# Four leading units instead of three in the gate/up stage of a two-layer trunk, with their first weights fetched and rounded inside the projection ahead

## The chip, the cores and the metric

The kernel runs on one NeuronCore of a Trainium2 chip. The time is device time of one execution in microseconds, the median of several. The engines are named as in the profile: PE (TensorE, matmuls), PEld (its weight loads), DVE (VectorE), ACT (ScalarE), POOL (GpSimd), SP (SyncE, which issues nearly all loads from HBM).

## The reference, cut to what matters

```
D_MODEL, SEQ, DEPTH, D_FF = 1024, 512, 2, 2816          # float32 throughout
def swiglu(x, w_gate, w_up, w_down):
    h = silu(x @ w_gate) * (x @ w_up)
    return h @ w_down
def reference(x, ...):
    h = x
    for i in range(DEPTH):
        m = diff_attention(h, ...) if i % 2 == 0 else short_gated_conv(h, ...)
        h = layer_norm(ALPHA * h + m, ln1_g[i], ln1_b[i])
        h = layer_norm(ALPHA * h + swiglu(h, w_gate[i], w_up[i], w_down[i]), ln2_g[i], ln2_b[i])
    return h
```

Each mixer ends in a projection of 1024 x 1024 (`wo` in layer 0, `wco` in layer 1), a residual and a layer norm. What follows it, gate and up of the SwiGLU, is what the change touches, in both layers.

## The kernel before, in words

Every matmul is done as three: an operand is split into a rounded part `hi` and the remainder `lo`, and hi·hi, hi·lo and lo·hi are added up in PSUM. So every weight tile is loaded raw and then made into a pair `whi`, `wlo`.

Gate and up run in 11 units (`UNITS`). A unit is one block of the Strassen-Winograd scheme: 7 products, 24 matmuls each (`product`, L580-L589), into three PSUM banks. Bank x takes x11·w11 and then x12·w21. Bank y takes s2·t2, s3·t3 and x22·t4. Bank z takes s1·t1 and s4·w22. The left factors (x11, x12, s1 to s4, x22) are made once in a layer from the normalized rows; w11, w12, w21, w22 are the four blocks of the unit's weights, and t1 to t4 are sums of them.

Two ways lead to a pair. A plain block (11, 21, 22) is loaded; ACT copies it to `whi` (L564) and its negative to `wlo` (L565), and POOL issues a DMA that adds the raw block to `wlo` (L566, called the accumulate below), after which `wlo` holds the remainder with its sign turned. A combined block (t1 to t4) is a sum on DVE (L576); ACT rounds it (L57), and DVE takes the remainder (L58).

The buffers are rings. Raw blocks 11 and 22 have three places (`raw`), 12 and 21 have two (`raw2`), `whi` and `wlo` have six each. The next load into a place waits until whatever read the old content is done; for a plain block that is the landing of its accumulate. SP issues loads strictly in its order, so a load that waits for its place holds those behind it.

The projection (`project_norm`, L203) works on four row tiles of 128 (tt = 0 to 3). The last four weight groups of its second half run tile by tile (L252), so that a tile's residual, norm and transposes can start while the next tile is multiplied. A `turn` (L168 to L198) transposes one row tile on PE (L175) and makes its part of the left factors on ACT and DVE: tiles 0 and 1 give x11 and x12, tiles 2 and 3 all the others, which need both halves. The turns of tiles 2 and 3 are left over to the next stage.

That stage (`swiglu`, L539) has `LEAD` = 3 leading units: for u = 0, 1, 2 the load of w11, the product x11·w11 and the copy `e` of bank x (`start`, L600, L608), with the turns of tiles 2 and 3 behind u = 0 and u = 1; then for the three units x12·w21 and a silu (`second`, L611); then the other five products of each (`rest`, L615). Units 3 to 10 do all seven products in one go. What stands after the leads is set by the order in which the kernel's text issues it and by a scheduler that orders each engine's list; the lists quoted below are what came out.

Of the kernel before, what the change touches and what calls it, by code (L numbers as in the profile page):

```python
# [35 lines left out]
LEAD = 3  # L36
# [3 lines left out]
def trunk(ctx: ExitStack, tc: tile.TileContext, t: dict):  # L40
# [113 lines left out]


# [12 lines left out]
    def turn_forms(tt, r, x, name):  # L168
# [20 lines left out]
        nc.scalar.copy(c, tps[0])  # L189
        nc.vector.tensor_tensor(d, a, tps[0], op=ALU.subtract)  # L190
        nc.vector.tensor_tensor(c, c, tps[1], op=ALU.add)
        form("s1", c)
        form("x22", tps[1])
        nc.vector.tensor_tensor(a, c, a, op=ALU.subtract)
        form("s2", a)
        form("s3", d)
        nc.vector.tensor_tensor(b, b, a, op=ALU.subtract)
        form("s4", b)  # L198
# [4 lines left out]
    def project_norm(lhs, w, kt, gb, xT, out, name, early=None):  # L203
# [335 lines left out]
    def swiglu(i, x, turns, open_next, out):  # L539
# [3 lines left out]
        with ExitStack() as fctx:  # L543
            wk = fctx.enter_context(tc.tile_pool(name=f"gu{i}", bufs=1, reuse_waits="tile"))

            def blocks(u, keys):
                out = {}
                for key in keys:
                    a, b = int(key[0]) - 1, int(key[1]) - 1
                    tag, pool, n = ("raw", wpool, 3) if a == b else ("raw2", wk, 2)  # L550
                    raw = pool.tile([P, 4, 256], F32, tag=tag, name=f"raw_gu{i}_{u}_{key}", bufs=n)
                    nc.sync.dma_start(raw, t["wgu"][i, u, a, b])
                    out[key] = raw
                return out

            def pair(name):
                hi = wpool.tile([P, 4, 256], F32R, tag="whi", name=f"whi_{name}")
                lo = wpool.tile([P, 4, 256], F32R, tag="wlo", name=f"wlo_{name}")
                return hi, lo


            def plain(raw, name):
                hi, lo = pair(name)
                nc.scalar.copy(hi, raw)  # L564
                nc.scalar.activation(lo, raw, AF.Copy, scale=-1.0)  # L565
                nc.gpsimd.dma_start(lo, raw, accum_op=ALU.add)  # L566
                return hi, lo
# [28 lines left out]
            def hidden(u):  # L596
                pool = slots["x"] if u >= UNITS - 4 else slots["xa"]
# [2 lines left out]
            def start(u, raw):  # L600
# [1 line left out]
                product(s["x"], plain(raw["11"], f"gu{i}_{u}_11"), "x11", True)
                if u < LEAD:
# [192 lines left out]
```

## Time and profile before

| | |
|---|---|
| median of 3 runs | 1150.58 us (1150.36 to 1151.18) |
| the profiled execution | 1150.07 us, span in the trace 1148.3 us |
| PE busy | 1119.0 us, 97% of the span |
| PEld / DVE / ACT / POOL busy | 999.1 / 737.4 / 520.8 / 119.6 us |
| PE clock granted, mean | 0.99 |
| accumulates `wlo_gu<-raw_gu` | 66, 512 KB each, median 5.8 us from issue to landing |
| loads `raw_gu<-in_wgu` | 100, 512 KB each, median 4.6 us |

Times in the rows are microseconds from the start of the span. A timeline row begins with start and duration; the bracket at its end, where there is one, holds how long the engine had stood idle before it and what ended that. In the rows of windows PEclk is the granted clock of TensorE (1.00 is 2.4 GHz, 0.50 is 1.2 GHz).

### The profile page before, as it was taken

How to read it: one execution, taken by the hardware profiler on the slowest of the kernel's cores; microseconds unless marked ns; L12 is line 12 of the kernel's file. 1: busy time of each engine (PE TensorE's matmuls, PEld its weight loads, DVE VectorE, ACT ScalarE, POOL GpSimd, SP SyncE). 2: the span in 40 equal slices, each digit the busy share in tenths (PEclk: the TensorE clock that was granted, in tenths of full speed). 3: DMA queues.
4: the chain of work that ended last, by engine and by line, in shares of the span. 5: the costliest groups of instructions: out<-in, count | busy, mean ns of one | idle time of the engine just before them, and what ended most of it. 6: DMA issues, size and time to landing. Idle time of an engine off the chain costs nothing.

```text
span 1148.3 us, 17876 instructions
## 1 busy us (share of the span) xinstructions
PE 1119.0 (97%) x7242; PEld 999.1 (87%) x7242; DVE 737.4 (64%) x1065; ACT 520.8 (45%) x790; POOL 119.6 (10%) x149
## 2 busy tenths in 40 slices
PE   9999999996999999999999999999899999999997
PEld 7877787786999999988889888889799999988886
DVE  7787877576986776832355544447897767682416
ACT  5554646536565655721212333225655565651210
POOL 1111112120011111000010000012001111100002
PEclk9999999998999999999999999999899999999998
DMA  8521222247788777533313423355778787743302
GB/s 290 178 74 37 74 60 89 76 111 199 189 204 194 173 201 176 150 96 106 111 56 111 146 92 92 94 155 120 216 196 193 177 191 186 164 137 101 106 24 74
DMA packets 44739, 155.58 MB, mean 135 GB/s; under 512 B 5200, under 2 KB 6096, under 8 KB 44656
## 3 DMA queue, kind: packets, MB, share of 16 engines
q1 hardware_dynamic: 35152, 119.83, 33.8%
q0 software_dynamic: 9504, 34.61, 16.5%
q8 instruction: 57, 0.93, 0.3%
q14 instruction: 26, 0.21, 0.1%
HBM read 117.72 MB, written 2.10 MB: 104 GB/s over the span
## 4 chain that ended last, share of the span: by engine, by line
PE 81%; DVE 6%; issue 4%; ACT 3%; DMA 3%; POOL 1%; SPq 0%; POOLq 0%; DVEq 0%; ACTq 0%
PE y L588 15%; PE z L588 10%; PE x L588 9%; PE o_dn L77 7%; PE o_dn L76 7%; PE o_dn L75 7%; PE in L75 4%; PE in L77 4%; PE in L76 4%; DMA wlo_gu<-raw_gu 2%; ACT p L426 1%; PE o_wco L75 1%; PE o_wco L77 1%; PE o_wco L76 1%; DVE nm L423 1%
## 5 line engine op out<-in xcount | busy, mean ns | idle before, releaser
L58 DVE TENSOR_TENSOR wlo_gu_t<-gu_t,whi_gu_t 128x1024 fp32r<-128x1024 f32 x88 | 106.9, 1221 | 30.4 <-ACT whi_gu_t L57 30.2
L58 DVE TENSOR_TENSOR wlo_dn<-raw_dn,whi_dn 128x1024 fp32r<-128x1024 f32 x44 | 53.6, 1222 | 112.6 <-ACT whi_dn L57 112.4
L57 ACT CAST whi_gu_t<-gu_t 128x1024 fp32r<-128x1024 f32 x88 | 90.9, 1047 | 75.3 <-DVE gu_t L576 29.6
L75 PE MATMUL o_dn<-whi_dn,hid 128*128 128x512 f32 (+1 forms) x320 | 123.8, 387 | 0.0
L77 PE MATMUL o_dn<-whi_dn,hid 128*128 128x512 f32 (+1 forms) x320 | 123.8, 387 | 0.0
L76 PE MATMUL o_dn<-wlo_dn,hid 128*128 128x512 f32 (+1 forms) x320 | 123.8, 387 | 0.0
L588 PE MATMUL x<-x_x_hi,wlo_gu 128*128 128x256 f32 x352 | 101.5, 288 | 9.6 <-DMA wlo_gu<-raw_gu 9.6
L57 ACT CAST whi_dn<-raw_dn 128x1024 fp32r<-128x1024 f32 x44 | 46.1, 1052 | 141.0 <-PE o_dn L77 107.5
L588 PE MATMUL x<-x_x_hi,whi_gu 128*128 128x256 f32 x352 | 101.7, 289 | 3.9 <-ACT lead L608 2.2
L566 POOL DMA_DIRECT2D wlo_gu<-raw_gu x66 | 57.5, 871 | 436.6 <-ACT wlo_gu L565 324.1
L588 PE MATMUL x<-x_x_lo,whi_gu 128*128 128x256 f32 x352 | 101.1, 287 | 0.0
L588 PE MATMUL y<-x_s_hi,wlo_gu_t 128*128 128x256 f32 x352 | 98.3, 279 | 0.2 <-DVE wlo_gu_t L58 0.2
L588 PE MATMUL y<-x_s_lo,whi_gu_t 128*128 128x256 f32 x352 | 98.4, 280 | 0.0
L588 PE MATMUL y<-x_s_hi,whi_gu_t 128*128 128x256 f32 x352 | 98.4, 279 | 0.0
L564 ACT CAST whi_gu<-raw_gu 128x1024 fp32r<-128x1024 f32 x66 | 69.2, 1050 | 62.7 <-PE y L588 28.4
L75 PE MATMUL in<-x_hi,whi_in 128*128 128x512 f32 (+1 forms) x240 | 83.7, 349 | 0.0
L77 PE MATMUL in<-x_hi,wlo_in 128*128 128x512 f32 (+1 forms) x240 | 83.2, 347 | 0.0
L76 PE MATMUL in<-x_lo,whi_in 128*128 128x512 f32 (+1 forms) x240 | 82.8, 345 | 0.0
L588 PEld LDWEIGHTS x<-x_x_hi,wlo_gu 128*128 128x128 f32 x352 | 68.9, 196 | 10.3 <-DMA wlo_gu<-raw_gu 10.3
L565 ACT ACTIVATE wlo_gu<-raw_gu 128x1024 fp32r<-128x1024 f32 x66 | 69.7, 1056 | 12.0 <-PE o_wco L76 8.7
L588 PEld LDWEIGHTS x<-x_x_hi,whi_gu 128*128 128x128 f32 x352 | 69.1, 196 | 4.5 <-ACT lead L608 2.4
L75 PEld LDWEIGHTS o_dn<-whi_dn,hid 128*128 128x128 f32 x320 | 60.2, 188 | 13.1
(237 smaller groups left out, 3104.5 us busy)
## 6 DMA issues: line engine op xcount, KB each, us to landing
raw_gu<-in_wgu SPq DMA_DIRECT2D x100, 512.0 KB, 4.6
wlo_gu<-raw_gu POOLq DMA_DIRECT2D x66, 512.0 KB, 5.8
raw_dn<-in_wdn SPq DMA_DIRECT2D x44, 512.0 KB, 3.7
raw_in<-in_win SPq DMA_DIRECT2D x24, 512.0 KB, 3.6
raw_qk<-in_wqk SPq DMA_DIRECT2D x14, 512.0 KB, 3.8
raw_v<-in_wv SPq DMA_DIRECT2D x8, 512.0 KB, 4.8
raw_wo<-in_wo SPq DMA_DIRECT2D x8, 512.0 KB, 3.7
raw_wco<-in_wco SPq DMA_DIRECT2D x8, 512.0 KB, 3.7
```

The lines of the kernel that those rows point to most:

```text
L57: nc.scalar.copy(hi, src)
L58: nc.vector.tensor_tensor(lo, src, hi.bitcast(F32), op=ALU.subtract)
L75: nc.tensor.matmul(out, lh, rh, start=first, stop=False)
L76: nc.tensor.matmul(out, lh, rl, start=False, stop=False)
L77: nc.tensor.matmul(out, ll, rh, start=False, stop=last)
L423: nc.vector.tensor_reduce(nm, ps[c][:, :n], axis=AX.X, op=ALU.max, negate=True)
L426: nc.scalar.activation(pc[:, :n], ps[c][:, :n], AF.Exp, bias=nm, accum_out=sm)
L564: nc.scalar.copy(hi, raw)
L565: nc.scalar.activation(lo, raw, AF.Copy, scale=-1.0)
L566: nc.gpsimd.dma_start(lo, raw, accum_op=ALU.add)
L588: nc.tensor.matmul(o, a, b[:, k, :], start=first and f + k + n == 0, stop=k == 3 and n == 2, skip_group_check=True)
```

## The change

`LEAD` becomes 4. `project_norm` gets a `fetch` that is called before its tile-by-tile part: it issues loads, copies and accumulates for w11 of all four units. The pairs of units 2 and 3 lie in a pool of their own (`hid_c`), not in the rings of six. The 21 blocks of the leads go through the `raw` ring of three. A turn of tile 2 or 3 now returns two functions: `soon` (row tile's differences, s2 and s1) and `later` (s3, x22, s4). The stage's order is written out by hand. The PE list becomes: x11·w11 of unit 0, transposes of tile 2, x11·w11 of unit 1, transposes of tile 3, x11·w11 of units 2 and 3, x12·w21 of units 0 to 3, then the five other products of unit 0 in the order s2·t2, s1·t1, s3·t3, s4·w22, x22·t4, of unit 1, and so on.

```diff
-LEAD = 3
+LEAD = 4
+    def fetch_gu(i):
+        lead[i] = []
+        for u in range(LEAD):
+            nm = f"gu{i}_{u}_11"
+            pair = None
+            if u >= 2:
+                pair = tuple(slot(slots["xb"], f"h{2 * u - 4 + j}", (4, 256), F32R, f"w{p}_{nm}")
+                             for j, p in enumerate(("hi", "lo")))
+            lead[i].append(plain(load_gu(i, u, "11", wpool, "raw", 3), nm, pair))
...
-        nc.scalar.copy(c, tps[0])
...
-        form("s4", b)
+        def soon():
+            nc.scalar.copy(c, tps[0])
+            nc.vector.tensor_tensor(d, a, tps[0], op=ALU.subtract)
+            nc.vector.tensor_tensor(c, c, tps[1], op=ALU.add)
+            nc.vector.tensor_tensor(a, c, a, op=ALU.subtract)
+            form("s2", a)
+            form("s1", c)
+        def later():
+            form("s3", d)
+            form("x22", tps[1])
+            nc.vector.tensor_tensor(b, b, a, op=ALU.subtract)
+            form("s4", b)
+        return soon, later
...
+        if fetch is not None:
+            fetch()
         for tt in range(NT):
...
-            for u in range(LEAD):
-                state[u] = start(u, blocks(u, ("11",)))
-                if u < 2:
-                    turns[u]()
-            for u in range(LEAD):
-                second(u, state[u], blocks(u, ("21",)))
+            def next21(u):
+                return plain(load_gu(i, u, "21", wpool, "raw", 3), f"gu{i}_{u}_21")
+            state, w2, later = [], [], []
+            state.append(start(0, lead[i][0]))
+            w2.append(next21(0))
+            keep(state[0])
+            soon = turns[0]()
+            w2.append(next21(1))
+            soon[0]()
+            later.append(soon[1])
+            state.append(start(1, lead[i][1]))
+            keep(state[1])
+            soon = turns[1]()
+            for u in range(2, LEAD):
+                state.append(start(u, lead[i][u]))
+            soon[0]()
+            later.append(soon[1])
+            raw = load_gu(i, 2, "21", wpool, "raw", 3)
+            raw0 = {key: load_gu(i, 0, key, wk, "raw2", 2) for key in ("12", "22")}
+            raw0.update(blocks(0, ("11",)))
+            keep(state[2])
+            w2.append(plain(raw, f"gu{i}_2_21"))
+            keep(state[3])
+            tw = sums(0, raw0)
+            w2.append(next21(3))
+            t1w = combined(tw[0], f"gu{i}_0_t1")
+            for f in later:
+                f()
             for u in range(LEAD):
+                second(state[u], w2[u])
+            raw0.update(blocks(0, ("21",)))
+            rest(0, state[0], raw0, tw, False, t1w)
+            for u in range(1, UNITS):
+                raw = blocks(u, ("11", "12", "22", "21"))
                 if u < LEAD:
+                    rest(u, state[u], raw, sums(u, raw), False)
...
```

`start` no longer copies (`keep` does), `sums` holds t1, t2 and the pair of t2, and `rest` takes them as arguments. `v_sb` moves to a pool that is released before `hid_c` is opened.

The lists below are those of layer 0; a name such as `gu0_2_11` means layer 0, unit 2, block 11, and the last number is the buffer's. ACT before, from the end of the `wo` projection on:

```order
L565 ACTIVATE wlo_gu0_1_11_2964<-raw_gu0_1_11_2960 128x1024
L564 CAST whi_gu0_1_11_2963<-raw_gu0_1_11_2960 128x1024
L57 CAST x1_x11_hi_2664<-tp_wo_0_0_2802 128x4x128
L57 CAST x1_x12_hi_2666<-tp_wo_0_1_2807 128x4x128
L185 COPY x1_raw_x11_2678<-tp_wo_0_0_2802 128x4x128
L187 COPY x1_raw_x12_2679<-tp_wo_0_1_2807 128x4x128
L565 ACTIVATE wlo_gu0_2_11_3023<-raw_gu0_2_11_3019 128x1024
L564 CAST whi_gu0_2_11_3022<-raw_gu0_2_11_3019 128x1024
L57 CAST x1_x11_hi_2664<-tp_wo_1_0_2854 128x4x128
```

and ACT after, at the same place:

```order
L173 CAST whi_gu0_2_11_2739<-raw_gu0_2_11_2741 128x1024
L174 ACTIVATE wlo_gu0_2_11_2740<-raw_gu0_2_11_2741 128x1024
L174 ACTIVATE wlo_gu0_1_11_2735<-raw_gu0_1_11_2732 128x1024
L173 CAST whi_gu0_1_11_2734<-raw_gu0_1_11_2732 128x1024
L173 CAST whi_gu0_3_11_2746<-raw_gu0_3_11_2748 128x1024
L174 ACTIVATE wlo_gu0_3_11_2747<-raw_gu0_3_11_2748 128x1024
L57 CAST x1_x11_hi_2671<-tp_wo_0_0_2837 128x4x128
L57 CAST x1_x12_hi_2673<-tp_wo_0_1_2842 128x4x128
L225 COPY x1_raw_x11_2685<-tp_wo_0_0_2837 128x4x128
L227 COPY x1_raw_x12_2686<-tp_wo_0_1_2842 128x4x128
```

Before, unit 2's rounding (L565, L564) stood behind the copies of row tile 0's forms; now the w11 of units 1, 2 and 3 are rounded ahead of them. Further on in the ACT list of after, where unit 3's w21 is rounded:

```order
L644 COPY lead0_2_3057<-x0_2_3032 128x512
L57 CAST whi_gu0_0_t2_3112<-gu0_0_t2_3110 128x1024
L57 CAST x1_s2_hi_2679<-x1_raw_x11_2685 128x4x128
L173 CAST whi_gu0_3_21_3118<-raw_gu0_3_21_3116 128x1024
L644 COPY e0_3_3083<-x0_3_3058 128x512
L174 ACTIVATE wlo_gu0_3_21_3119<-raw_gu0_3_21_3116 128x1024
L57 CAST whi_gu0_0_t1_3123<-gu0_0_t1_3108 128x1024
```

The copy to `whi` of unit 3's 21 stands behind the rounding of t2, and the copy to its `wlo` behind `keep` of unit 3 (L644). The DVE list of after, ahead of that rounding of t2:

```order
L611 TENSOR_TENSOR gu0_0_t1_3108<-raw_gu0_0_12_3095,raw_gu0_0_11_3099 128x1024
L234 TENSOR_TENSOR x1_raw_x11_2685<-x1_raw_x21_2687,x1_raw_x11_2685 128x4x128
L58 TENSOR_TENSOR x1_s1_lo_2676<-x1_raw_x21_2687,x1_s1_hi_2675 128x4x128
L232 TENSOR_TENSOR x1_raw_s3_2688<-x1_raw_x11_2685,tp_wo_3_0_3022 128x4x128
L58 TENSOR_TENSOR x1_s2_lo_2680<-x1_raw_x11_2685,x1_s2_hi_2679 128x4x128
L233 TENSOR_TENSOR x1_raw_x21_2687<-x1_raw_x21_2687,tp_wo_3_1_3027 128x4x128
L611 TENSOR_TENSOR gu0_0_t2_3110<-raw_gu0_0_22_3097,gu0_0_t1_3108 128x1024
```

The sum t2 stands behind t1 and five operations on forms. SP's loads before, from the first leads on:

```order
L552 DMA raw_gu0_0_11_3149<-in_wgu 128x1024
L552 DMA raw_gu0_0_22_3153<-in_wgu 128x1024
L552 DMA raw_gu0_1_11_3320<-in_wgu 128x1024
L552 DMA raw_gu0_0_21_3053<-in_wgu 128x1024
L552 DMA raw_gu0_1_21_3085<-in_wgu 128x1024
L114 DMA g_f0_5589<-in_ln2_g 128x1024
L115 DMA b_f0_5590<-in_ln2_b 128x1024
L552 DMA raw_gu0_2_21_3117<-in_wgu 128x1024
L552 DMA raw_gu0_0_12_3151<-in_wgu 128x1024
```

and after:

```order
L162 DMA raw_gu0_2_21_3093<-in_wgu 128x1024
L162 DMA raw_gu0_0_11_3099<-in_wgu 128x1024
L162 DMA raw_gu0_0_12_3095<-in_wgu 128x1024
L162 DMA raw_gu0_0_22_3097<-in_wgu 128x1024
L162 DMA raw_gu0_3_21_3116<-in_wgu 128x1024
L114 DMA g_f0_5601<-in_ln2_g 128x1024
L162 DMA raw_gu0_1_11_3394<-in_wgu 128x1024
L162 DMA raw_gu0_1_22_3398<-in_wgu 128x1024
L115 DMA b_f0_5602<-in_ln2_b 128x1024
L162 DMA raw_gu0_2_11_3565<-in_wgu 128x1024
L162 DMA raw_gu0_0_21_3241<-in_wgu 128x1024
L162 DMA raw_gu0_1_12_3396<-in_wgu 128x1024
```

Before, unit 1's second load of block 11 stood ahead of the 21 of units 0 and 1; now the 21s of units 0 to 2 come first (units 0 and 1 just above this piece), and unit 2's second load of 11 stands directly ahead of 0_21 and 1_12. DVE before, in the first unit's five products:

```order
L576 TENSOR_TENSOR gu0_0_t4_3254<-raw_gu0_0_21_3155,gu0_0_t2_3159 128x1024
L58 TENSOR_TENSOR wlo_gu0_0_t3_3226<-gu0_0_t3_3223,whi_gu0_0_t3_3225 128x1024
L623 TENSOR_TENSOR u20_0_3190<-lead0_0_2933,y0_0_3161 128x512
L576 TENSOR_TENSOR gu0_1_t1_3328<-raw_gu0_1_12_3322,raw_gu0_1_11_3320 128x1024
L58 TENSOR_TENSOR wlo_gu0_0_t4_3289<-gu0_0_t4_3254,whi_gu0_0_t4_3288 128x1024
L627 TENSOR_TENSOR w50_0_3221<-lead0_0_2933,z0_0_3192 128x512
L576 TENSOR_TENSOR gu0_1_t2_3330<-raw_gu0_1_22_3324,gu0_1_t1_3328 128x1024
```

and after:

```order
L611 TENSOR_TENSOR gu0_0_t3_3297<-raw_gu0_0_22_3097,raw_gu0_0_12_3095 128x1024
L58 TENSOR_TENSOR x1_s4_lo_2684<-x1_raw_x12_2686,x1_s4_hi_2683 128x4x128
L58 TENSOR_TENSOR wlo_gu0_0_t3_3300<-gu0_0_t3_3297,whi_gu0_0_t3_3299 128x1024
L611 TENSOR_TENSOR gu0_0_t4_3328<-raw_gu0_0_21_3241,gu0_0_t2_3110 128x1024
L58 TENSOR_TENSOR wlo_gu0_0_t4_3363<-gu0_0_t4_3328,whi_gu0_0_t4_3362 128x1024
L663 TENSOR_TENSOR u20_0_3268<-lead0_0_2961,y0_0_3243 128x512
L611 TENSOR_TENSOR gu0_1_t1_3402<-raw_gu0_1_12_3396,raw_gu0_1_11_3394 128x1024
L611 TENSOR_TENSOR gu0_1_t2_3404<-raw_gu0_1_22_3398,gu0_1_t1_3402 128x1024
L667 TENSOR_TENSOR w50_0_3295<-lead0_0_2961,z0_0_3270 128x512
```

In the list of after u20_0, which empties bank y, stands behind t4 and its remainder; w50_0 stands behind t1 and t2 of unit 1.

## Rows read from the trace of the kernel before

**Rows 1.** The page's first lines: span, and busy time of each engine.

```profile
span 1148.3 us, 17876 instructions
...
PE 1119.0 (97%) x7242; PEld 999.1 (87%) x7242; DVE 737.4 (64%) x1065; ACT 520.8 (45%) x790; POOL 119.6 (10%) x149
```

**Rows 2.** PE's waits: line, waited for, us in total, times, longest.

```profile
PE x L588 <- DMA wlo_gu<-raw_gu: 9.6, 3, 5.0
...
PE x L588 <- ACT lead L608: 2.2, 1, 2.2
...
PE z L588 <- DMA wlo_gu<-raw_gu: 1.9, 2, 1.3
...
PE x L588 <- ACT whi_gu L564: 1.7, 1, 1.7
...
PE y L588 <- DVE wlo_gu_t L58: 0.2, 1, 0.2
```

**Rows 3.** Timeline of PE, layer 0, leading units: start, duration, idle before.

```profile
250.08 0.28 PE L588 MATMUL x<-x_x_hi,whi_gu 128*128 128x256 f32 x1
...
252.91 1.03 PE L175 MATMUL tp_wo<-ident,res 128*128 128x128 f32 x8
...
253.70 0.36 PE L588 MATMUL x<-x_x_hi,whi_gu 128*128 128x256 f32 x1
...
265.74 0.58 PE L588 MATMUL x<-x_x_hi,wlo_gu 128*128 128x256 f32 x1 [5.02 <-DMA wlo_gu<-raw_gu]
...
272.94 0.39 PE L588 MATMUL x<-x_x_hi,whi_gu 128*128 128x256 f32 x1 [1.71 <-ACT whi_gu L564]
...
278.69 0.58 PE L588 MATMUL x<-x_x_hi,wlo_gu 128*128 128x256 f32 x1 [2.66 <-DMA wlo_gu<-raw_gu]
...
297.87 0.28 PE L588 MATMUL y<-x_s_hi,whi_gu_t 128*128 128x256 f32 x1
```

**Rows 4.** Timeline of PE, layer 1, the same stage.

```profile
789.42 0.28 PE L588 MATMUL x<-x_x_hi,whi_gu 128*128 128x256 f32 x1
...
807.68 0.52 PE L588 MATMUL x<-x_x_hi,whi_gu 128*128 128x256 f32 x1 [2.21 <-ACT lead L608]
...
810.31 0.58 PE L588 MATMUL x<-x_x_hi,wlo_gu 128*128 128x256 f32 x1 [1.90 <-DMA wlo_gu<-raw_gu]
...
831.12 0.28 PE L588 MATMUL y<-x_s_hi,whi_gu_t 128*128 128x256 f32 x1
```

**Rows 5.** Chain of waits, stretches 245 to 300 and 800 to 830: start, duration, what.

```profile
247.42 4.63 DMA wlo_gu<-raw_gu
...
252.48 4.58 DMA raw_gu<-in_wgu
...
259.92 5.78 DMA wlo_gu<-raw_gu
...
818.62 6.93 DMA wlo_gu<-raw_gu
```

**Rows 6.** Windows: PE, PEld, DVE, ACT, POOL busy (x count), PE clock granted, DMA.

```profile
266.00:271.30 5.30, 5.22 (x24) 4.93 (x24) 1.69 (x3) 2.80 (x4) 0.85 (x1) 0.50 0.85 196
...
312.15:326.30 14.15, 14.15 (x123) 14.15 (x122) 14.12 (x16) 8.58 (x10) 1.71 (x2) 1.00 0.87 208
```

**Rows 7.** Timeline of ACT, layer 0: a copy to wlo, and a copy e.

```profile
245.07 1.06 ACT L565 ACTIVATE wlo_gu<-raw_gu 128x1024 fp32r<-128x1024 f32 x1 [0.65 <-PE o_wo L76]
...
253.11 0.59 ACT L608 COPY lead<-x 128x512 f32<-128x512 f32 x1 [2.38 <-PE x L588]
```

**Rows 8.** Timeline of DVE, layer 0: a form's sum, and a weight sum.

```profile
255.79 0.68 DVE L191 TENSOR_TENSOR x_raw_x<-x_raw_x,tp_wo 128x512 f32<-128x512 f32 x1
...
275.71 1.23 DVE L576 TENSOR_TENSOR gu_t<-raw_gu,raw_gu 128x1024 f32<-128x1024 f32 x1 [3.04 <-DMA raw_gu<-in_wgu]
```

**Rows 9.** Source view of L566, the accumulates: its last line.

```profile
DMA to landing us min/median/max: 4.5/5.8/10.1
```

**Rows 10.** Source view of L552, the loads of gate/up blocks: its last line.

```profile
DMA to landing us min/median/max: 3.4/4.6/8.5
```

More of the change, by code (lines that the diff above doesn't have):

```diff
@@ L151, in norm_tile, with open_gu, load_gu, pair_gu @@
         return turn
+    def open_gu(i):
+        slots["x"] = right_pool(f"hid_b{i}")
+        slots["xb"] = right_pool(f"hid_c{i}")
+    def load_gu(i, u, key, pool, tag, n):
+        a, b = int(key[0]) - 1, int(key[1]) - 1
+        raw = pool.tile([P, 4, 256], F32, tag=tag, name=f"raw_gu{i}_{u}_{key}", bufs=n)
+        nc.sync.dma_start(raw, t["wgu"][i, u, a, b])
+        return raw
+    def pair_gu(name):
+        hi = wpool.tile([P, 4, 256], F32R, tag="whi", name=f"whi_{name}")
+        lo = wpool.tile([P, 4, 256], F32R, tag="wlo", name=f"wlo_{name}")
+        return hi, lo
+    def plain(raw, name, pair=None):
+        hi, lo = pair or pair_gu(name)
+        nc.scalar.copy(hi, raw)
+        nc.scalar.activation(lo, raw, AF.Copy, scale=-1.0)
+        nc.gpsimd.dma_start(lo, raw, accum_op=ALU.add)
+        return hi, lo
+    def fetch_gu(i):
[4 more added lines that the diff above has]
+            if u >= 2:
+                pair = tuple(
+                    slot(slots["xb"], f"h{2 * u - 4 + j}", (4, 256), F32R, f"w{p}_{nm}")
+                    for j, p in enumerate(("hi", "lo"))
+                )
+            lead[i].append(plain(load_gu(i, u, "11", wpool, "raw", 3), nm, pair))
+    lead = {}
     HOME = {"x11": (8, 9), "x12": (10, 11), "s1": (12, 13), "x22": (0, 1), "s2": (2, 3), "s3": (4, 5), "s4": (6, 7)}
@@ L188, in turn_forms, with project_norm @@
             return
-        nc.scalar.copy(c, tps[0])
[L190 to L197, printed above, removed]
-        form("s4", b)
-    def project_norm(lhs, w, kt, gb, xT, out, name, early=None):
+        def soon():
[11 more added lines that the diff above has]
+        return soon, later
+    def project_norm(lhs, w, kt, gb, xT, out, name, early=None, fetch=None):
         ng = kt // GROUP
@@ L546, in blocks @@
             def blocks(u, keys):
[L547 to L567, printed above, removed]
+                return {
+                    key: load_gu(i, u, key, *((wpool, "raw", 3) if key[0] == key[1] else (wk, "raw2", 2)))
+                    for key in keys
+                }
             def combined(raw, name):
-                hi, lo = pair(name)
+                hi, lo = pair_gu(name)
                 split(hi, lo, raw)
@@ L596, in hidden, with start @@
             def hidden(u):
[L597 removed]
+                pool = slots["xb" if u < 4 else "xa" if u < UNITS - 4 else "x"]
                 return slot(pool, f"h{u}", (2, S), F32, f"h{i}_{u}")
[L600 removed]
+            def start(u, w):
                 s = {"x": bank(f"x{i}_{u}")}
[L602 to L603 removed]
+                product(s["x"], w, "x11", True)
+                if u < 3:
                     both = slot(slots["xa"], f"h{UNITS - 5 - u}", (2, 512), F32, f"lead{i}_{u}")
@@ L628, in rest @@
                 if whole:
-                    second(u, s, raw)
+                    second(s, plain(raw["21"], nm + "21"))
                 t3 = tsum(raw["22"], raw["12"], ALU.subtract, nm + "t3")
```

48 lines of the change are left out of this document (27 added, 21 removed).

## The prediction

> **What bounds the kernel now.** The page's first lines come first: PE is busy 97% of the span [rows 1], so only what makes PE wait or run slowly can be won. Next PE's waits: on the products of gate and up it waits 9.6 us for accumulates, 2.2 for a copy `e`, 1.7 for a copy to `whi`, 1.9 for accumulates in bank z, 0.2 on DVE [rows 2]. That is 15.6 us; the reader is to see that almost all of it stands in this stage. Third, the timeline of PE there. In layer 0 the first leading product starts at 250.08 and unit 1's first y product at 297.87, 47.79 us later [rows 3]; in layer 1 it is 789.42 to 831.12, 41.70 us [rows 4]. What it would be without a wait is read from the same rows: the product from 250.08 to 252.91 takes 2.83 us and a turn's transposes from 252.91 to 253.70 take 0.79 [rows 3]. Between the two marks lie 3 + 3 + 5 = 11 products and 2 turns: 11 x 2.83 + 2 x 0.79 = 32.7. So 15.1 us are lost in layer 0 and 9.0 in layer 1, 24.1 in all. Of these 15.6 are the waits. The other 8.5 are PE at half its clock: after the waits of 5.02 and 2.66 matmuls take longer (0.58 instead of 0.28 in the rows that end those waits), and from 266.00 to 271.30 the granted clock is 0.50, 24 matmuls in 5.30 us [rows 3, 6]. In layer 1 the same is seen after the 2.21 us wait [rows 4]. After the wait of 1.71 the row reads 0.39 [rows 3], nearer to full speed. 24.1 us is the most that can be won here. After this stage nothing changes in kind: a unit takes 14.15 us with PE and clock full, though DVE is busy 14.12 of these [rows 6].
>
> **The change, part by part.** New positions without waits, layer 0, by the 2.83 and 0.79 above: x11·w11 of the units at 250.08, 253.70, 257.32 and 260.15; x12·w21 at 262.98, 265.81, 268.64 and 271.47; unit 0's five products from 274.30 on; unit 1's y at 288.45. Unit 3's two products (5.66 us) are done early and come back later, so they cost nothing.
>
> First, the fetch. Unit 2's w11 was rounded late because its ring place was freed only by the projection: the copy at 245.07 waits for an `o_wo` matmul [rows 7]. With own places for units 2 and 3, and the roundings ahead of tile 0's forms in ACT's list, all four are ready before 250. They lie beside the projection's last tiles, where PE is full and ACT is not; cost nothing, and if that cover failed one ACT pair (2 x 1.06 [rows 7]) would delay the forms of x11 by as much.
>
> Second, the 21s. Before, SP held 0_21 and 1_21 behind a load that waited for the accumulate that landed at 252.05; then 4.58 us of load, a wait for ACT, and 5.78 of accumulate ended PE's 5.02 us wait at 265.7 [rows 3, 5]. Now POOL's place at 247.42 [rows 5] holds 0_21's accumulate, which lands about 252.05, needed at 263.2. 1_21's follows; even with the longest accumulate in the trace, 10.1 [rows 9], and two issues it is there by 260, needed at 266. 2_21's is issued about 254 behind the last norm's operations on POOL and lands by 264.1, needed at 268.9. The waits of 5.02, 1.71, 2.66 in layer 0 and 2.21, 1.90 in layer 1 go with the half clock after them.
>
> Third, what is late next: 3_21's accumulate. ACT rounds 3_21 behind the rounding of t2 and writes `wlo` behind `keep` of unit 3. t2 needs unit 0's 11, 12 and 22 again; SP gets to 11 when 0_21's accumulate lands, 252.05, and 12 is there about 257.1, as the load issued in that second place now is (252.48 + 4.58 [rows 5]). On DVE t1, five form operations and t2 follow: 1.23 + 5 x 0.68 + 1.23 = 5.9 [rows 8], so 263.0. On ACT come whi of t2, a form, whi of 3_21, `keep`, wlo: 3 x 1.06 + 2 x 0.59 = 4.4 [rows 7], so 267.4, POOL issues about 267.5. The durations overlap a little at both engines, hops add a little; I leave both out. Needed is the remainder at the third matmul of unit 3's second product, 271.7. With 4.5, 5.8 and 10.1 to landing [rows 9] the wait is 0.3, 1.6 or 5.9. I take 6.4, between 5.78 and 6.93 [rows 5], since loads are in flight as in those two: landing 273.9, wait 2.2.
>
> The Trainium skill (DMA: Bandwidth & Descriptors, section "Anatomy of one DMA — SWDGE (gpsimd) path") has a fit of about 2.0 us plus the bytes over 436e3 per us, which for 512 KB gives, as an estimate, 3.2 us. No accumulate here is that short, the shortest of 66 takes 4.5 [rows 9]; by the page 3_21 would land at 270.7, in time in both layers; the third and fourth steps and the sixth would cost nothing, 1.0 a layer would stay lost, and the time would be 1128.5, below case B. I go by the rows.
>
> Fourth, the chain behind that landing, call it L. SP's list has unit 2's second 11 in the ring place of 3_21, so it waits for L, and 0_21 stands behind it. 0_21 is there at L + 0.4 + 4.6 [rows 10]; t4 1.23, its whi 1.06, its wlo 1.23 follow, and u20_0, 0.68, stands behind them on DVE [rows 7, 8]: L + 9.2. u20_0 must have emptied bank y before s3·t3 may start, and PE is there at L + 22 matmuls of the product that waited (2.6) and two products (5.7): L + 8.3. Wait 0.9 to 1.1. In the same way 1_12, t1 and t2 of unit 1 stand ahead of w50_0: L + 5.0 + 1.2 + a load of 3.4 to 4.6 [rows 10] + 3.1, so L + 12.7 to 13.9, against L + 12.1 for s4·w22. I take 0.9. Together 2.0 in each layer; if those waits were hidden by anything slower, nothing.
>
> Fifth, DVE. Its list has nine large and seven small operations in a unit's period; with 1.14 and 0.60 back to back that is 14.5 against PE's 14.15, an estimate from 14.12 of 14.15 busy [rows 6]. Bound: nothing to 0.5 per unit; I take 0.33 for three units, 1.0 per layer.
>
> Sixth, the clock. After a wait of 2.2 it fell in layer 1, after 1.71 it hardly did [rows 3, 4]. A half-clock stretch costs up to 3.4 (the 8.5 are two such and a half one), but while PE is slow the 2.0 of the fourth step vanish. I put 0.6 for layer 0, bounds 0 and 1.4.
>
> Layer 1: the same lists. POOL's issue and L are not bound by layer 0's rows; the wait lies between none and layer 0's 2.2, I take 1.1.
>
> Sum lost: layer 0 2.2 + 2.0 + 1.0 + 0.6 = 5.8; layer 1 1.1 + 2.0 + 1.0 = 4.1; 9.9 of the 24.1 stay, 14.2 are won. The profiled execution took 1150.07, of which 1148.3 are the span [rows 1] and 1.8 lie around it and stay: 1135.9. The median of the runs is 0.5 above the profiled one: about 1136.
>
> **The rivals.** A, above, its own range 1132 to 1141.
> B: 3_21 lands in time or nearly, the chain waits do not form, only DVE's 1.0 a layer and about 2 more are lost: 24.1 - 4 = 20.1, so 1130. For it: 4.5 us accumulates exist and operations overlap. Against: the median 5.8 is already late by 1.6.
> C: accumulates of 8 us and more, since more transfers run at once, and DVE bound by 0.5 a unit: two waits of 4, a half-clock stretch in each layer in place of the chain (3.4), 1.5 a layer on DVE: 2 x 8.9, about 17.5 lost, 6.6 won, 1144. For it: the longest is 10.1 [rows 9], and DMA share is 0.85 already in a window here [rows 6].
> D, slower: SP's list. Each microsecond that 3_21 lands later moves 0_21, t4, u20_0 and all of PE behind it by one, in both layers. To eat 14.2 it takes 7.1 in each, so an accumulate of 13.5 us; at 15 it is 1136 + 2 x 8.5 = 1153. Against: 10.1 is the longest of 66.
> E: the change does not do what it says: the early fetch delays the projection by what it saves, or the waits only move, around 1150. Against: the projection's raw loads all stand ahead of the fetch in SP's list, and ACT has room before 245.07, where it stands idle 0.65 for PE [rows 7].
>
> **How the numbers follow.** A 0.55, B 0.20, C 0.17, D 0.04, E 0.04. Predicted 1136. The range goes from 1129 to 1146: it holds A, most of B, C, and leaves out D, E and the ends of B and C, under 2 in 10. 0.2%, about 2.3 us, is what a measurement of this kernel can tell from no change; A, B and C lie beyond it on the fast side: faster 0.92, E same 0.04, D slower 0.04.
>
> **What would show it.** Right: in PE's waits no accumulate in x but one, in unit 3's second product, of 1 to 3 us; unit 1's y at about 293 in layer 0; short waits of y for u20_0 and of z for w50_0; DVE full from there to unit 3. Wrong: waits on x11·w11 of units 2 or 3 (the fetch), a wait above 5 on 3_21, or a longer time from tile 0's norm to 250.08, which would mean that the fetch disturbs the projection.

## The result, and the profile after

The changed kernel takes 1137.61 us (median of 4 runs, 1133.89 to 1139.12), the kernel before 1150.47 beside it (4 runs, 1149.53 to 1151.18): ratio 0.9884, 95% interval 0.9859 to 0.9909. Predicted were 1136, range 1129 to 1146. The profiled execution took 1137.30. One slip in the account of the kernel before: `wlo` holds the remainder with its plain sign, since the accumulate adds raw to -hi.

The page's first lines, against [rows 1]:

```profile
span 1135.5 us, 17877 instructions
PE 1113.9 (98%) x7242; PEld 994.1 (88%) x7242; DVE 736.3 (65%) x1065; ACT 522.1 (46%) x790; POOL 118.6 (10%) x149
```

The span is 12.8 shorter. PE's busy time fell by only 5.1 of these. The number of matmuls is the same, so they ran faster on average, which fits fewer of them at half clock; the rest is idle time that went. PE's waits (line, waited for, total, times, longest), against [rows 2]:

```profile
PE x L623 <- DMA wlo_gu<-raw_gu: 4.3, 2, 2.8
...
PE z L623 <- DVE w L667: 1.6, 2, 0.8
PE y L623 <- DVE u L663: 1.3, 2, 1.1
```

Of 9.6 us for accumulates in x, 4.3 are left, one wait in each layer. The waits for `e`, for `whi` and for accumulates in bank z are gone. New are two of z and two of y, for the DVE sums that empty these banks: w50_0 (L667) and u20_0 (L663).

PE's timeline (start, duration, what; in the bracket the idle time before it) of both layers, against [rows 3, 4]: the first leading product, the rows with waits, unit 1's first y product, and unit 4's first product.

```profile
250.51 0.28 PE L623 MATMUL x<-x_x_hi,whi_gu 128*128 128x256 f32 x1
...
274.99 0.38 PE L623 MATMUL x<-x_x_hi,wlo_gu 128*128 128x256 f32 x1 [2.77 <-DMA wlo_gu<-raw_gu]
...
288.60 0.35 PE L623 MATMUL z<-x_s_hi,whi_gu 128*128 128x256 f32 x1 [0.75 <-DVE w L667]
...
294.37 0.28 PE L623 MATMUL y<-x_s_hi,whi_gu_t 128*128 128x256 f32 x1
...
337.53 0.28 PE L623 MATMUL x<-x_x_hi,whi_gu 128*128 128x256 f32 x1
...
781.02 0.28 PE L623 MATMUL x<-x_x_hi,whi_gu 128*128 128x256 f32 x1
...
804.30 0.39 PE L623 MATMUL x<-x_x_hi,wlo_gu 128*128 128x256 f32 x1 [1.56 <-DMA wlo_gu<-raw_gu]
...
813.88 0.36 PE L623 MATMUL y<-x_s_hi,whi_gu_t 128*128 128x256 f32 x1 [1.06 <-DVE u L663]
...
817.75 0.36 PE L623 MATMUL z<-x_s_hi,whi_gu 128*128 128x256 f32 x1 [0.81 <-DVE w L667]
...
823.52 0.28 PE L623 MATMUL y<-x_s_hi,whi_gu_t 128*128 128x256 f32 x1
...
866.69 0.28 PE L623 MATMUL x<-x_x_hi,whi_gu 128*128 128x256 f32 x1
```

From the first leading product to unit 1's y there are now 13 products and 2 turns, 13 x 2.83 + 2 x 0.79 = 38.37 without waits. Layer 0 took 294.37 - 250.51 = 43.86, so 5.49 are lost; layer 1 took 42.50, so 4.13. The next three units take 43.16 and 43.17 against 3 x 14.15 = 42.45: another 0.71 and 0.72. Together 6.20 and 4.85, 11.05 of the 24.1 us; 13.05 are won, and 1150.07 - 13.05 = 1137.0 is the profiled time to within 0.3. Little is won or lost elsewhere: from the first leading product to the first matmul of the down projection layer 0 is 8.8 shorter than before and layer 1 4.1, which is the span's 12.8 to within 0.1.

The windows (PE, PEld, DVE, ACT, POOL busy with counts, granted clock, DMA share), against [rows 6]: the first leading products beside the last row tile's norm, the stretch behind them with the wait for 3_21 (block 21 of unit 3), the rest of the product that waited in layer 0 and in layer 1, and units that wait for nothing.

```profile
250.00:260.00 10.00, 10.00 (x85) 9.88 (x85) 6.22 (x11) 6.99 (x12) 3.43 (x4) 1.00 0.98 215
260.00:277.50 17.50, 14.73 (x119) 14.54 (x119) 16.63 (x22) 13.49 (x19) 0.87 (x1) 0.94 0.84 254
274.99:279.30 4.31, 4.31 (x23) 4.31 (x24) 1.95 (x3) 3.44 (x4) 0.30 (x1) 0.60 0.72 241
804.30:807.10 2.80, 2.80 (x23) 2.80 (x24) 1.23 (x1) 2.80 (x4) 0.00 (x0) 1.00 0.63 168
870.00:990.00 120.00, 120.00 (x1021) 120.00 (x1020) 83.04 (x90) 71.40 (x81) 15.57 (x19) 1.00 0.78 180
```

DVE is busy 6.22 of the first 10 us and 16.63 of the 17.5 behind them: it stands idle for loads and is then full. The DMA share in the first window is 0.98. After the wait of 2.77 the mean granted clock is 0.60, most of the stretch at 0.50 and the rest at 1.00, and 23 matmuls take 4.31; after 1.56 it stays at 1.00 and 23 take 2.80. The chain of waits there (start, duration, what), against [rows 5]:

```profile
250.67 4.99 DMA wlo_gu<-raw_gu
255.71 10.63 DMA raw_gu<-in_wgu
...
270.05 4.89 DMA wlo_gu<-raw_gu
```

1_21's accumulate lands at 255.66 and frees the place for 3_21's load, which takes 10.63, to 266.34. ACT rounds t2 and then 3_21, and at 270.05 3_21's accumulate is issued, the one that PE waits for.

### The profile page after: what moved, and what is told of

Same layout as the page of the kernel before. It is cut to its first block, busy times and chain, and to the rows that moved or that the text cites. A ratio compares the mean times of both kernels' runs of the same rounds, so it can differ in the third digit from the quotient of the medians.

```text
span 1135.5 us, 17877 instructions
## 1 busy us (share of the span) xinstructions
PE 1113.9 (98%) x7242; PEld 994.1 (88%) x7242; DVE 736.3 (65%) x1065; ACT 522.1 (46%) x790; POOL 118.6 (10%) x149
## 4 chain that ended last, share of the span: by engine, by line
PE 73%; DVE 11%; DMA 5%; issue 4%; ACT 4%; POOL 2%; SPq 0%; POOLq 0%; DVEq 0%; ACTq 0%
PE y L623 14%; PE z L623 9%; PE x L623 7%; PE o_dn L77 7%; PE o_dn L76 7%; PE o_dn L75 7%; PE in L75 4%; PE in L77 4%; PE in L76 4%; DMA raw_gu<-in_wgu 3%; DMA wlo_gu<-raw_gu 2%; ACT p L476 1%; DVE nm L473 1%; DVE gu_t L611 1%; PE o_wo L75 1%
## 5 line engine op out<-in xcount | busy, mean ns | idle before, releaser
L623 PE MATMUL x<-x_x_hi,whi_gu 128*128 128x256 f32 x352 | 99.4, 282 | 0.0
L76 PEld LDWEIGHTS o_dn<-wlo_dn,hid 128*128 128x128 f32 x320 | 60.2, 188 | 13.1
L77 PEld LDWEIGHTS o_dn<-whi_dn,hid 128*128 128x128 f32 x320 | 60.1, 188 | 13.0
L75 PEld LDWEIGHTS o_dn<-whi_dn,hid 128*128 128x128 f32 x320 | 60.2, 188 | 13.0
```

Source lines behind the costliest of these rows:

```text
L75: nc.tensor.matmul(out, lh, rh, start=first, stop=False)
L76: nc.tensor.matmul(out, lh, rl, start=False, stop=False)
L77: nc.tensor.matmul(out, ll, rh, start=False, stop=last)
L623: nc.tensor.matmul(o, a, b[:, k, :], start=first and f + k + n == 0, stop=k == 3 and n == 2, skip_group_check=True)
```

## The experiments

In what follows "late forms" are s3, x22 and s4 of a tile (`later`).

**The changed kernel again.**

> The changed kernel once more, as the base for the others on this chip: 1134 to 1139, with the accumulate of unit 3's 21 late by 1 to 3 us in each layer. If the spread of its four runs (1133.9 to 1139.1) comes from that landing and from the clock that falls or does not fall behind it, a run with a shorter wait there has full clock in layer 0 and is about 3 us faster; if it comes from elsewhere, the wait there is the same and another stretch is longer.

Median 1138.18 (1133.43 to 1139.46, 4 runs), ratio 0.9889 (0.9849 to 0.9928). The profiled run was the quick one, and its accumulate waits are those of before it, 3.08 and 1.47. Its window of layer 1's later units:

```profile
870.00:990.00 120.00, 120.00 (x1061) 120.00 (x1060) 87.15 (x94) 75.16 (x85) 16.40 (x19) 1.00 0.81 185
```

That is 1061 matmuls where the first profile had 1021, at the same granted clock and with PE busy throughout in both: a whole unit of seven products takes 19.04 us instead of 19.79. So what made this run quick is not the landing of 3_21, as the first half of the expectation had it, but another stretch, as the second half had it.

**Three leads in the new order, with own places.**

```diff
-LEAD = 4
+LEAD = 3
```

and the lines for unit 3 (`keep(state[3])`, `next21(3)`) are left out.

> Three leading units instead of four, all else as changed (early fetch, own place for unit 2's pair, 21s first, forms in two parts). Theory: the gain comes from the loads' order and the own places, the fourth unit only puts off its own accumulate; then no accumulate is waited for in bank x, u20 stands ahead of t4 on DVE, and the time is that of the changed kernel within 2 us, 1135 to 1139. Rival: the fourth unit's 2.8 us products are the cover that lets the accumulates land; then 2_21 is waited for by 2 to 5 us in each layer and the time is 1141 to 1146.

1139.42 (1138.51 to 1140.24), ratio 0.9907 (0.9873 to 0.9941). No accumulate is waited for in x. What is waited for in its place (PE starts at 277.78, u20_0 ended at 277.63, so it is the emptying of bank y that decides, not the copy that the row names):

```profile
PE y L623 <- ACT wlo_gu L174: 5.1, 2, 3.2
```

The time is 0.4 above the expected range. By the medians (1137.61 and 1138.18 with four leads) the fourth lead brings 1.2 to 1.8 us, but the ranges overlap, so that it brings anything is not shown. With four, u20_0 is waited for less (1.3 in all) and an accumulate is late instead.

**Four leads without own places.**

```diff
-            if u >= 2:
+            if u >= LEAD:
```

> Four leading units, but the pairs of units 2 and 3 lie in the rings of six instead of in places of their own. Theory: the ring places come free only with the projection's last weights (about 245 to 247), so 2_11, 3_11 and behind them 0_21 and 1_21 are accumulated one after the other from 247 on; waits of 3 to 6 us on bank x in each layer, with half clock behind them, 1144 to 1152. Rival: the cover of four units suffices anyway; then within 2 us of the changed kernel.

1152.11 (1149.74 to 1155.11, 10 runs), ratio 1.0021 (1.0002 to 1.0040): the whole gain is gone.

```profile
PE x L623 <- DMA wlo_gu<-raw_gu: 17.6, 6, 6.2
```

Six waits for accumulates are back. ACT's roundings stand for PE again, which frees the ring places: the one at 246.08 0.65 us for a matmul of the projection, the one at 258.00 4.18 us for a product of gate and up. Without own places the early fetch is worth nothing.

**The kernel before with an own place for unit 2's w11, and nothing else.** The pool gets its place by a move of `v_sb` to a pool that is released earlier.

```diff
-                product(s["x"], plain(raw["11"], f"gu{i}_{u}_11"), "x11", True)
+                own = tuple(slot(slots["xb"], f"h{j}", (4, 256), F32R, f"w{p}_gu{i}_{u}_11")
+                            for j, p in enumerate(("hi", "lo"))) if u == 2 else None
+                product(s["x"], plain(raw["11"], f"gu{i}_{u}_11", own), "x11", True)
```

> The kernel before with one part of the change alone: unit 2's first pair in a place of its own, so its rounding no longer waits for the projection's weights. Loads, their order and the three leads as before. Theory: the second needed part is where the 21s are loaded to; before, they go to a pool whose memory opens only when the projection has ended (about 250), so 0_21 is accumulated at 263 to 265 at best in place of 265.7; only the 1.71 and part of the 5.02 go: 1145 to 1149. Rival: SP's wait for 2_11's accumulate (252.05) was the cause of all that followed; with it gone layer 0's 15 us go, 1134 to 1141.

1147.94 (1142.01 to 1149.09, 10 runs), ratio 0.9973 (0.9949 to 0.9997): about 3 us.

```profile
PE x L591 <- DMA wlo_gu<-raw_gu: 4.7, 3, 2.0
PE y L591 <- ACT whi_gu_t L57: 4.6, 1, 4.6
```

In x the accumulate waits are halved (9.6 to 4.7), and a wait of 4.6 for the rounding of a weight sum appears, which the kernel before did not have.

**The new order with three leads, pairs in the rings.** Both edits of the second and third experiment.

> The other part alone: the changed order of loads with 21s in the ring of the projection and forms in two parts, three leads, and no place of its own for unit 2's pair. Theory: the two parts need each other; 2_11's rounding waits for a ring place until about 245 to 247, POOL's list and the ring of raw blocks put the 21s behind it, and waits of 3 to 6 us on bank x return: 1145 to 1152. Rival: the order is enough: within 2 us of the run with three leads, 1137 to 1142.

1148.04 (1143.16 to 1151.02, 10 runs), ratio 0.9990 (0.9966 to 1.0014).

```profile
PE z L623 <- DMA wlo_gu<-raw_gu: 5.4, 2, 2.9
PE y L623 <- DVE wlo_gu_t L58: 4.3, 4, 1.4
PE x L623 <- DMA wlo_gu<-raw_gu: 2.1, 2, 1.7
```

The time is as expected; the waits are spread over x, y and z rather than on x. Places alone bring about 3, the order alone nothing that stands clear of zero, both with three leads 10.7 (0.0093 x 1150): the parts need each other.

**Left factors made in one part.**

```diff
-            later.append(soon[1])
+            soon[1]()
```

(at both turns)

> The forms of tiles 2 and 3 in one part again (s3, x22, s4 directly behind s2 and s1 of the tile); all else as changed. DVE's list then has ten form operations ahead of t2 instead of five, so ACT's rounding of t2, of 3_21 behind it and the accumulate come some 3 us later, and the wait on unit 3's 21 grows from 2.8 and 1.6 to 4 to 7; in return t3 and t4 find DVE free and u20 is not waited for. Theory: the two nearly cancel, 1138 to 1141. Rival: the split is a main part of the gain; then 1143 or more.

1141.36 (1139.80 to 1142.99), ratio 0.9931 (0.9911 to 0.9951). About 3 us more than the changed kernel, a little above the 1138 to 1141 of the first theory.

```profile
PE x L623 <- DMA wlo_gu<-raw_gu: 6.4, 2, 3.7
PE x L623 <- ACT whi_gu L173: 3.0, 2, 2.6
```

Both the rounding and the accumulate of a 21 come late, and nothing waits for u20_0, as expected.

**t1 and t2 behind the late forms.**

```diff
-            tw = sums(0, raw0)
 ...
-            t1w = combined(tw[0], f"gu{i}_0_t1")
             for f in later:
                 f()
+            tw = sums(0, raw0)
+            t1w = combined(tw[0], f"gu{i}_0_t1")
```

> The sums t1, t2 of unit 0 and their pairs are issued behind the late forms instead of ahead of them; all else as changed. Theory: DVE is full there, so what is put behind is late: t3, t4 and u20 follow t2, bank y's s3·t3 waits 4 to 6 us in each layer, while 3_21's accumulate, no longer behind t2, comes in time or 1 us late: 1139 to 1143. Rival: the accumulate alone matters; then 1132 to 1135.

1146.23 (1144.46 to 1147.42, 10 runs), ratio 0.9966 (0.9955 to 0.9977). Slower than either theory said, in the place that the first one named:

```profile
PE y L623 <- DVE u L663: 8.9, 3, 5.1
PE x L623 <- DMA wlo_gu<-raw_gu: 5.3, 2, 3.3
```

The y waits grow as expected, and the accumulate stays late as well (3.3 and 2.05), which was not.

**3_21's remainder on DVE, so without an accumulate.**

```diff
-            w2.append(next21(3))
+            w2.append(combined(load_gu(i, 3, "21", wpool, "raw", 3), f"gu{i}_3_21"))
```

> The remainder of unit 3's 21 is made on DVE by one subtraction instead of by copy and accumulate; all else as changed. The wait on x12·w21 of unit 3 (2.77 and 1.56 us) goes under both theories. Theory: the next wait takes its place, since 0_21 is loaded into a place that is free only after t3, t4 follows and u20 stands behind t4; then bank y's s3·t3 waits 2 to 4 us and the time falls by 0 to 2 only, 1135 to 1138. Rival: the chain behind that landing goes with it, and the time falls by 4 to 7, 1130 to 1133.

1138.94 (1137.50 to 1144.49, 6 runs), ratio 0.9912 (0.9884 to 0.9940). Unit 3's second product waits no more, and nothing is won. The profiled execution is the slowest of the six (1144.49), with a wait of 2.66 for a copy `e` in a later unit of layer 1; the row is from its layer 0:

```profile
285.51 0.55 PE L623 MATMUL y<-x_s_hi,whi_gu_t 128*128 128x256 f32 x1 [4.70 <-DVE u L663]
```

The next wait takes the place of the one removed: s3·t3 waits 4.70 for u20_0, and its 0.55 shows PE at half clock (0.50 granted from 285.5 to 289).

**The same, with three places for 12 and 21.**

```diff
-                    key: load_gu(i, u, key, *((wpool, "raw", 3) if key[0] == key[1] else (wk, "raw2", 2)))
+                    key: load_gu(i, u, key, *((wpool, "raw", 3) if key[0] == key[1] else (wk, "raw2", 3)))
```

(and unit 0's 12 and 22 likewise; `e` has one place to make room)

> As the run with unit 3's remainder on DVE, and the ring for 12 and 21 has three places instead of two (paid for by one place instead of two for the copy e). Theory: in the former run bank y's s3·t3 waited 4.7 and 2.6 us for u20, because SP could issue 0_21 only when t3 had released its place (274.7), so t4 was late and u20 stands behind t4 on DVE. With a third place 0_21 is there early; what is left is DVE's own queue, and u20 comes 1 to 3 us earlier: 1134 to 1137. Rival: DVE's list alone makes u20 late (forms, t1 to t4 and their remainders, full from 260 to 277); then the wait stays and the time is 1138 to 1140.

1137.01 (1135.16 to 1138.21), ratio 0.9897 (0.9875 to 0.9919): the time stands between the theory's and the rival's.

```profile
283.56 0.55 PE L623 MATMUL y<-x_s_hi,whi_gu_t 128*128 128x256 f32 x1 [3.96 <-DVE u L663]
```

0_21 no longer waits for a place, and u20_0 is still late. DVE stands idle 2.76 us for a load ahead of t1, and from then to u20_0 (282.73) only 0.45 and 0.77 more. So what is left to hold u20_0 is DVE's list and the loads at its head.

**Further, POOL takes two remainders and a sum of the late forms, and t3 is made early.**

```diff
-            form("s3", d)
+            form_g("s3", d)
             form("x22", tps[1])
-            nc.vector.tensor_tensor(b, b, a, op=ALU.subtract)
-            form("s4", b)
+            nc.gpsimd.tensor_tensor(b, b, a, op=ALU.subtract)
+            form_g("s4", b)
```

(`form_g` takes the remainder on POOL; `tsum(raw0["22"], raw0["12"], ...)` for t3 follows t2)

> As the run before this one, and in addition the sum t3 of unit 0 directly behind t1 and t2, and five-eighths of the late forms' work off DVE: the remainders of s3 and s4 and the sum under s4, both row tiles, on POOL (six operations of 128x512, 1.3 to 1.5 us each there as its other products of that size show). If DVE's queue and the place of 0_21 are all that is left, no wait above 0.5 us stands between the first leading product and unit 1's y: of the changed kernel's 2.77, 0.75, 1.56, 1.07, 0.81 and the 1.5 of half clock nothing stays, 8.5 us in all: 1128 to 1132. Rival: POOL's operations take longer than 1.5 us beside DVE's, or slow DVE's; then bank z's s4·w22 waits for s4, and the time is 1134 or more.

1138.40 (1136.49 to 1139.80), ratio 0.9904 (0.9883 to 0.9925): no gain. The rival was right in the time and in POOL's slowing DVE's operations, but PE waits elsewhere than it said, for 3_21's remainder and for u20_0, both made on DVE:

```profile
PE x L627 <- DVE wlo_gu L58: 4.8, 2, 2.6
PE y L627 <- DVE u L667: 4.1, 2, 2.7
```

DVE's timeline and POOL's beside it:

```profile
264.37 2.36 DVE L615 TENSOR_TENSOR gu_t<-raw_gu,gu_t 128x1024 f32<-128x1024 f32 x1 [0.85 <-DMA raw_gu<-in_wgu]
...
267.86 2.32 DVE L615 TENSOR_TENSOR gu_t<-raw_gu,raw_gu 128x1024 f32<-128x1024 f32 x1
...
270.70 1.21 DVE L58 TENSOR_TENSOR wlo_gu_t<-gu_t,whi_gu_t 128x1024 fp32r<-128x1024 f32 x1
271.84 2.28 DVE L58 TENSOR_TENSOR wlo_gu<-raw_gu,whi_gu 128x1024 fp32r<-128x1024 f32 x1
```

```profile
264.36 1.29 POOL L242 TENSOR_TENSOR x_s_lo<-x_raw_s,x_s_hi 128x512 fp32r<-128x512 f32 x1
...
267.41 1.68 POOL L245 TENSOR_TENSOR x_raw_x<-x_raw_x,x_raw_x 128x512 f32<-128x512 f32 x1 [1.76 <-DVE x_raw_x L234]
...
271.31 1.73 POOL L242 TENSOR_TENSOR x_s_lo<-x_raw_x,x_s_hi 128x512 fp32r<-128x512 f32 x1 [2.22 <-ACT x_s_hi L241]
```

Each large DVE operation that begins behind one of POOL takes 2.3 us; the one that begins ahead of its POOL neighbour (270.70) takes 1.21, and that neighbour 1.73. The three end 1.08, 1.09 and 1.08 after their POOL neighbour (266.73 against 265.65, and so on), about an operation's own time, as if DVE worked only once POOL was done. The Trainium skill (SBUF — State Buffer, "Who interferes with whom") says that a DVE instruction with two inputs in SBUF contends with a GpSimd one that reads SBUF, that the ports they share are an exclusive lock, and that the order of issue decides which of the two is blocked. These rows agree, 2.36 - 1.21 = 1.15 beside a POOL operation of 1.29. Two edits went in together here, so what the early t3 did to the time is not separated.

**t3 early and three places, the accumulate kept.** The ring and the t3 edit of the last two, without POOL's part and with `next21(3)` as in the changed kernel.

> As changed, with the sum t3 of unit 0 directly behind t1 and t2, and three places for 12 and 21 (one for the copy e); accumulate for 3_21 kept, nothing on POOL. SP then issues 0_21 without waiting for t3 or for 3_21's landing. Theory: the landing of 3_21 stays late (2.8 and 1.6 us), the waits for u20 and w50 (0.75, 1.07, 0.81) go: 2 to 3 us less, 1134 to 1136. Rival: u20 now stands behind t1, t2 and t3 of unit 1 on DVE's list and takes the place of what went: 1138 to 1142.

1140.86 (1140.40 to 1142.45, 8 runs), ratio 0.9932 (0.9910 to 0.9954). The time is the rival's, the mechanism neither's:

```profile
PE x L623 <- DMA wlo_gu<-raw_gu: 11.0, 2, 6.9
```

Nothing waits for u20_0; the accumulate itself is late (6.87 and 4.16). POOL issued it at 269.40, no later than in the changed kernel (270.05), but it took 8.90 for 4.89 (in layer 1 7.23 for 5.44). The stretch from 269.40 to 274.30, in the changed kernel and then in this one:

```profile
269.40:274.30 4.90, 2.82 (x25) 2.62 (x24) 4.90 (x8) 4.41 (x7) 0.87 (x1) 1.00 0.89 238
```

```profile
269.40:274.30 4.90, 2.09 (x19) 1.89 (x17) 4.90 (x8) 4.87 (x7) 0.87 (x1) 1.00 1.02 329
```

The DMA engines move 329 GB/s where they moved 238 (last column). In the changed kernel SP waits for the landing with its next load, to 275.00; with a third place it sends another at 267.35, and this one, with the last norm loads (under way to 272.38 and 274.31), runs beside the accumulate. As far as this run shows, the freed place is paid for with a slower transfer.

**3_21 loaded ahead of unit 0's blocks, its remainder on DVE, tile 2's late forms ahead of t1, three places.**

```diff
+            raw3 = load_gu(i, 3, "21", wpool, "raw", 3)
 ...
+            later.pop(0)()
             tw = sums(0, raw0)
-            w2.append(next21(3))
+            w2.append(combined(raw3, f"gu{i}_3_21"))
```

> As the run with three places for 12 and 21 and unit 3's remainder on DVE, with DVE's list turned round: unit 3's 21 is loaded ahead of unit 0's second 11, 12 and 22, and the late forms of tile 2 stand ahead of t1. In the runs so far DVE stood idle for 2.5 to 3 us (256.3 to 259) because t1, whose loads land at 259 to 264, stood ahead of forms that were ready. Theory: DVE's list in this stage is what is left of the wait; with forms done while the loads land, u20 comes 2 to 3 us earlier than in that run (283.4), and the waits for u20 (3.96, 2.54, 0.94) shrink to 0 to 1.5 each: 1130 to 1134. Rival: DMA is what is left, the loads of 11, 12 and 22 land later by as much as they are issued later (10 us each when five are in flight), t2 and with it everything behind it moves back: 1137 to 1141.

1130.95 (1130.11 to 1131.93, 6 runs), ratio 0.9842 (0.9807 to 0.9877): faster than both kernels, as expected. Its waits, and two stretches:

```profile
PE y L623 <- DVE u L663: 2.0, 2, 1.1
...
PE x L623 <- DVE wlo_gu L58: 0.5, 1, 0.5
```

```profile
250.00:260.00 10.00, 10.00 (x87) 9.92 (x86) 9.17 (x16) 7.30 (x13) 3.44 (x4) 1.00 0.97 222
...
850.00:970.00 120.00, 120.00 (x1021) 120.00 (x1021) 86.03 (x92) 69.71 (x78) 15.60 (x18) 1.00 0.78 184
```

DVE is busy 9.17 of the 10 us where it was 6.22: the late forms run while the loads of 12 and 11 are under way. What the rival said of the loads is true as well: t1 starts at 265.98, for 259.10 with three places alone, and still waits 1.90 for its load. Even so u20_0 ends at 281.96, 1.45 earlier than there (not 2 to 3), and PE, which itself comes to it 1.4 later, waits 1.12 for it instead of 3.96. The granted clock is 1.00 from 250.3 to 290.8, where it had been 0.50 behind the 3.96. Loads and DVE's list were changed together; which of the two carries the gain was not separated. From the first leading product to the down projection it is 222.0 and 220.7 us, against 225.5 and 224.2 in the changed kernel: 3.5 in each layer. The second row shows that this is not a profile in which the units ran at the quicker pace.

## Why the prediction was right, step by step

Case A came in, at 1137.6 for 1136: layer 0 lost 6.20 for 5.8, layer 1 4.85 for 4.1.

First, the fetch: right. No wait on x11·w11 of units 2 and 3, and the stage starts at 250.51 for 250.08 before; from tile 0's norm (DVE's aggregate at 234.04, for 233.62 before) to there it is 16.47 for 16.46, so the fetch does not disturb the projection. Four leads without own places show that these carry it.

Second, the 21s: right. 0_21, 1_21 and 2_21 are not waited for, nor the half clock after them. 2_21's accumulate took 11.2 and landed at 265.39, for "by 264.1", and needed to be there at 268.9.

Third, 3_21: the wait is 2.77 for 2.2 and 1.56 for 1.1. In layer 0 that is luck, two errors that nearly cancel; layer 1's 1.1 was a choice between bounds and not a sum. The loads were taken at 4.58. With up to six transfers under way at once, 0_12's took 6.89, to 259.84, and 0_22's 10.28, to 264.44. DVE stood for both, ahead of t1 and ahead of t2:

```profile
259.94 1.23 DVE L611 TENSOR_TENSOR gu_t<-raw_gu,raw_gu 128x1024 f32<-128x1024 f32 x1 [3.04 <-DMA raw_gu<-in_wgu]
...
264.47 1.22 DVE L611 TENSOR_TENSOR gu_t<-raw_gu,gu_t 128x1024 f32<-128x1024 f32 x1 [0.30 <-DMA raw_gu<-in_wgu]
```

So t2 was done at 265.69, for 263.0, and POOL could issue at 270.05, for 267.5. 3_21's own load, which the prediction left out, landed at 266.34, only 0.86 before ACT came to it (267.20): with t2 in time it would have held POOL until about 269.2 by itself, an estimate from ACT's 2.85 us between there and POOL's issue. The landing then took 4.89 for 6.4; few loads ran beside it (the run with t3 early and three places shows 8.90 where more do). So the term that failed is the loads' duration, 6.9 to 10.6 for 4.6, and the 6.4 made up for it. The sources' last lines, against [rows 9, 10], show how far both kinds reach (first the accumulates, then all loads of gate and up blocks, then the 4 of them issued from 252 to 257):

```profile
DMA to landing us min/median/max: 4.5/5.9/11.2
...
DMA to landing us min/median/max: 3.4/4.6/10.6
...
DMA to landing us min/median/max: 5.5/8.6/10.6
```

Fourth, the chain behind it: 1.06 + 0.81 = 1.87 in layer 1, for 2.0. In layer 0 u20_0 ended at 284.13, which is L + 9.2 as worked out; the wait on it did not form because PE was slow, as step six had it, and 0.75 on w50_0 is left. That it exists is shown with 3_21's remainder on DVE: that wait gone, u20_0 is waited for 4.70. That it hangs on the landing, as L + 9.2 has it, is only half of the truth: with three places as well, neither an accumulate nor a ring place stands ahead of 0_21 any more, and u20_0 still comes 3.96 late, by DVE's list. What nearly cured it was to change that list's order and the loads' together.

Fifth, DVE: 0.71 and 0.72 for 1.0, inside its bound. In layer 0 DVE is busy 42.25 of these 43.16 us, which fits; that DVE sets the pace there is not isolated by a run. Where PE had lost more ahead of them (t3 early and three places), the same three units took 14.13 each.

Sixth, the clock: 1.53 for 0.6 in layer 0 (22 matmuls in 4.39, where 22 behind a short wait took 2.86 at full clock before), a little above the bound of 1.4; nothing in layer 1, as taken.

Of the first stretch 0.44 and 0.70 are in no row of waits and were not traced further.

The rivals: B fell with the 2.77; C's late accumulates came, of 11.2, but on 2_21, which had the room for it (its 2 x 8.9 is 17.8 and not 17.5, which moves C by 0.3). E, that the changed kernel does not do what it says, is what four leads without own places look like. D needed 7.1 more in each layer; 3_21 landed 1.0 later than forecast (274.94 for 273.9).

## What to carry to other kernels

A wait that stands in the shadow of another costs nothing until that other one is removed, so after each one removed look for what is late next, in the order of each engine's list: here the accumulate, then u20_0, then almost nothing. Where an engine is idle for a load at the head of its list and full behind it, put work that is ready first: here that, with the loads' order, gave 6 us, and giving DVE less work by way of POOL gave nothing. Take a transfer's duration from rows in which as many transfers are under way as in the new place.

## What was not expected of the hardware

Transfers that run together: with up to six of 512 KB under way between 252.5 and 266.3, two loads of blocks took 10.3 and 10.6 us and an accumulate 11.2, where medians are 4.6 and 5.9, and 8.5 and 10.1 were the most before [rows 9, 10]. The same accumulate of 3_21 took 4.89 at 238 GB/s and 8.90 at 329.

VectorE beside GpSimd: 2.3 us instead of 1.21 for an operation that begins behind one of GpSimd, in the rows of the experiment with POOL.

TensorE's pace: in 2 of 14 profiles the units of one layer took 19.04 us instead of 19.79, with PE busy throughout and 1.00 granted in both. 0.75 us in each of 7 or 8 units is 5 to 6 us in a layer, which is about the size of the differences between runs of one kernel (the kernel before from 1140.0 to 1154.2 over the whole study, the changed one from 1133.4 to 1139.5). What sets it was not found, and that it makes the whole spread is not shown; a difference below 1% between single runs says nothing here.
